# Zero-padding the 64-row and 33-row matmuls of a two-block sequence model to 128 rows, with two more pages of SBUF

## The chip, the cores and the metric

One core of a Trainium2 chip runs the whole program. The metric is the device time of one execution in microseconds; the kernel before was run three times, with a median of 2347.4 us. A core has TensorE (matmuls into PSUM, each preceded by a load of its stationary operand), VectorE, ScalarE and GpSimd (elementwise work), and a queue, SyncE, that issues most of the DMAs. SBUF has 128 partitions; a matmul contracts over the partitions, so "rows" below means the partitions that its two operands span.

## What is computed

512 tokens of width 1024 (float32) go through two blocks of two layers each. Cut to what the change touches, the reference is

```python
# first block, each layer: h = rmsnorm(x) @ w_in, cut into heads
#   sliding-window attention with sinks: 4 query heads of 64, 2 key heads of 64
scores = einsum('bnqhgd,bnkhd->bnhgqk', qb, kk) * (d ** -0.5)
#   stick-breaking attention: 4 heads of 64
z = einsum('bqhd,bkhd->bhqk', qblk, kf) * scale
# second block, each layer: 8 query heads and 2 key heads of 64, 512 tokens and 256 context tokens
s = einsum('bqhgd,bkhd->bhgqk', q, k) * (HEAD_DIM ** -0.5)
# second block's long convolution: its filter comes from a small network over 33 position features
h = sin(fr1 * (z @ w1 + b1));  h = sin(fr2 * (h @ w2 + b2));  h = h @ w3     # 33 -> 64 -> 64 -> 512
```

The rest is projections, a latent attention, a gated convolution, Fourier mixing, the modulation of the second block by a condition, and convolved feed-forward halves.

## The kernel before

The program is one straight list of instructions, traced from Python generators that `weave` interleaves: attention steps beside projections that fill TensorE. A scheduler then sets each engine's order from the instructions' dependences, so neighbours in the code are not always neighbours on TensorE.

Large products are split products (`mm3`, lines 559 to 561): each float32 operand is held as a high and a low part of a type that TensorE takes in one pass, and three matmuls over 128 rows give high*high, high*low and low*high. Small products are done directly in float32, which the trace shows as two passes each.

Heads have 64 features, so some products span 64 rows:

- `stick` (line 924): two heads stand in the two halves of the partitions of one tile, keys `qk[2 * pr + 1]` and queries `qk[2 * pr]`; head `hh` uses rows `64 * hh` to `64 * hh + 64` of both.
- `swa` (line 1060): the two key heads are the two halves of one tile; query head `h` uses half `h // 2`.
- `filter_nets` (line 1172) contracts over the 33 position features, then over 128 rows that hold both layers' hidden units; `filters` (line 1198) takes one layer's 64 rows.
- `Mix.attend` (lines 1892 and 1893), the second block's scores: queries are stored as high and low parts stacked on the partitions, and the high keys `kh` twice over, so one 128-row matmul (line 1892) gives both parts of the query times the high key. The low keys `kl` are stored once, two heads in the two halves, and a 64-row matmul (line 1893) adds the high query times the low key into the same PSUM bank. There are 8 (query tile, head pair) steps for the context, one key segment each, and in each layer 16 for the tokens, with a segment of 512 and one of 256 keys; each step has two heads, which makes 144 matmuls on each of the two lines. Behind the scores come VectorE's maximum (line 1897), ScalarE's exponential (line 1898), transposes of the weights on TensorE (line 1919), copies out of PSUM (line 1924), and the products with the values (`pv_pair`, lines 886 and 887), which put two heads side by side in two halves of TensorE's columns.

The modulation's products (line 1303) use a quarter of the columns each. `Mix.keys` (line 1716 on) makes `kh`, `kl` and the values of a token tile; line 1736 copies `kl`. `dense` makes the first block's queries and keys, one ScalarE copy out of PSUM for each tile of 128 features.

SBUF is handed out by `Arena`: 24 pages of columns, `PAGES`, each of which holds one type at a time. A first trace records when each buffer is needed, `place` assigns pages and columns, and `spread` moves buffers so that there is a pause before columns are used again. GpSimd does the `rstd` of every norm (lines 568 and 569), two small instructions in its queue.

Of the kernel before, what the change touches and what calls it, by code (L numbers as in the profile page):

```python
# [12 lines left out]
ALU = mybir.AluOpType  # L13
# [15 lines left out]
# ---------------------------------------------------------------- first block: column layout  # L29
# [20 lines left out]
def tiles_a(w, cols):  # L50
    """[K, N] -> [len(cols), 128, K/128 * 128]: one column group of 128 in each unit."""
    k = w.shape[0] // P
    out = w[:, np.concatenate([np.asarray(c) for c in cols])]
    out = out.reshape(k, P, len(cols), P).transpose(2, 1, 0, 3)
    return np.ascontiguousarray(out.reshape(len(cols), P, k * P))


def tiles_b(w, per):
    """[K, N] -> [K/128/per, 128, per * N]: `per` row groups of 128 in each unit."""
# [5 lines left out]
def cols128(v):  # L65
    """[n * 128] -> [128, n]"""
# [28 lines left out]
# The second block's input projection, by feature: queries, keys, values, the Fourier part, and the  # L95
# six tiles of the long convolution in the order in which they are used.
# [7 lines left out]
def dft_tables():  # L104
    """Tables that depend on the shapes alone: transforms, filter positions and decay, rotations."""
    out = {}
    f = np.float32
    for tag, n in (("x", S), ("c", C)):
        nt = n // P
        ht = nt // 2  # L110
        # Odd multiples of half a bin, by halves: the frequencies k and n - 1 - k share all but signs,
        # and even and odd times go apart.
# [3 lines left out]
        # [frequency tile, time in the tile, time tile, (re, im), frequency]  # L116
        fwd = np.stack([np.cos(ang), -np.sin(ang)]).reshape(2, ht, P, nt, P).transpose(1, 4, 3, 0, 2)
        out["fwd_" + tag] = np.ascontiguousarray(fwd.reshape(ht, P, nt * 2 * P).astype(f))
        if n == S:
            # [frequency tile, frequency, (re, im), time]  # L120
            inv = np.stack([np.cos(ang), -np.sin(ang)]).reshape(2, ht, P, n).transpose(1, 2, 0, 3)
        else:
            # [frequency or its mirror, frequency, (re, im), time]
# [14 lines left out]
        out["hyz_" + tag] = np.ascontiguousarray(z.T.astype(f))  # L138
# [21 lines left out]
def pack2(g, a):  # L160
# [5 lines left out]
    # What the modulation's rows take: the bias, and for the two gates the gains that go with them.  # L166
# [16 lines left out]
    # Both layers' filter networks side by side.  # L183
    hw = np.zeros((P, 772), f)
    for l in two:
# [3 lines left out]
        hw[ls, 260:772] = g["hy_w3_2"][l]  # L189
# [30 lines left out]
def pack(inp):  # L220
    """Lays the inputs out for the chip: no arithmetic."""
# [37 lines left out]
def weave(*streams):  # L259
    """Traces generators side by side: next comes the one that is least far on. A stream is a  # L260
    generator of costs and their expected sum."""
# [15 lines left out]
PAGES = [2048] * 23 + [720]  # L277
# [14 lines left out]
class Arena:  # L292
    """Columns of SBUF, handed out and taken back as the program is traced: what is read and written
# [1910 lines left out]
```

## Time and profile before

| | |
|---|---|
| runs | 2347.40, 2346.09, 2356.58 us, median 2347.4 us |
| profiled execution: span of its instructions | 2345.5 us; its own time is not given apart, the median of the runs is 1.9 us above the span |
| TensorE busy | 2251.5 us, 96% |
| VectorE, ScalarE, GpSimd busy | 1409.6, 1017.0 and 219.5 us |
| granted TensorE clock, mean | 0.982 of full speed |
| DMA | 235.33 MB, 100 GB/s |

Busy time counts the union of an engine's instructions. The ends of matmuls are modelled, and neighbours overlap in the records, so for TensorE the distance from one start to the next tells more than a duration does. PE is TensorE, PEld its weight loads, DVE VectorE, ACT ScalarE, POOL GpSimd. In a matmul's shape "64*128 64x512" the first number is the rows, the second the columns of the stationary operand, the last the columns that stream.

### The profile page before, as it was taken

To read this page: it belongs to the slowest core of one execution; us is meant where nothing else is said; L and a number is where in the kernel's file an instruction comes from. 1 tells how busy PE (TensorE), PEld (TensorE's weight loads), DVE (VectorE), ACT (ScalarE), POOL (GpSimd) and SP (SyncE) were. 2 spreads that over 40 slices of the span, in tenths; PEclk is the share of its full clock that TensorE was granted. 3 is DMA by queue.
4 is the path that set the end of the run, shared out by engine and by line. 5 is a ranking of instruction groups with operands and counts; after the bars stand their busy time and mean duration, and the time that the engine had idled before them with its cause. 6 is when DMAs were issued, how large, how long until landed. Compare 5 with 4: busy or idle time off the path is not lost.

```text
span 2345.5 us, 31203 instructions
## 1 busy us (share of the span) xinstructions
PE 2251.5 (96%) x12119; PEld 1755.1 (75%) x12122; DVE 1409.6 (60%) x2480; ACT 1017.0 (43%) x1896; POOL 219.5 (9%) x368
## 2 busy tenths in 40 slices
PE   7999999999999989999999999999889999999997
PEld 6545678755577777678988888888677778888886
DVE  4665675346666465565755655655866556566565
ACT  4345444255346335665532332223545555433332
POOL 1052002021012100010000000000320001000001
PEclk9989999999999989999999999999899999999999
DMA  5566423455531123213211221212134022233221
GB/s 167 184 205 195 154 85 93 132 177 175 158 110 54 55 68 124 88 47 116 76 56 45 81 72 54 72 54 83 46 108 135 28 89 83 73 107 108 99 90 63
DMA packets 72396, 235.33 MB, mean 100 GB/s; under 512 B 9046, under 2 KB 11031, under 8 KB 72248
## 3 DMA queue, kind: packets, MB, share of 16 engines
q1 hardware_dynamic: 65392, 223.06, 29.4%
q10 hardware_dynamic: 6856, 10.27, 1.4%
q8 instruction: 95, 1.56, 0.3%
q14 instruction: 53, 0.43, 0.1%
HBM read 224.82 MB, written 8.49 MB: 99 GB/s over the span
## 4 chain that ended last, share of the span: by engine, by line
PE 60%; DVE 6%; DMA 4%; ACT 3%; POOL 2%; issue 1%; DVEq 0%; POOLq 0%; ACTq 0%; SPq 0%
PE f L560 9%; PE f L559 9%; PE f L561 9%; PE b L559 7%; PE b L561 7%; PE b L560 7%; PE f L1893 2%; PE b L1919 2%; PE f L1892 2%; DVE page L528 2%; PE b L887 2%; POOL small L569 1%; ACT page L527 1%; PE b L886 1%; DMA page<-b_up 1%
## 5 line engine op out<-in xcount | busy, mean ns | idle before, releaser
L527 ACT ACTIVATE page<-page 128x1024 fp32r<-128x1024 f32 (+7 forms) x472 | 393.3, 846 | 631.9 <-PE f L560 158.1
L528 DVE TENSOR_TENSOR page<-page,page 128x1024 fp32r<-128x1024 f32 (+7 forms) x472 | 450.4, 967 | 324.5 <-ACT page L527 308.7
L559 PE MATMUL f<-page,page 128*128 128x512 f32 (+2 forms) x1456 | 522.4, 361 | 11.5 <-ACT page L527 10.7
L560 PE MATMUL f<-page,page 128*128 128x512 f32 (+2 forms) x1452 | 525.2, 362 | 6.5 <-DVE page L528 6.4
L561 PE MATMUL f<-page,page 128*128 128x512 f32 (+2 forms) x1452 | 519.3, 359 | 0.0
L559 PE MATMUL b<-page,page 128*128 128x512 f32 (+3 forms) x1352 | 511.5, 379 | 6.1 <-ACT page L527 2.0
L560 PE MATMUL b<-page,page 128*128 128x512 f32 (+3 forms) x1356 | 503.4, 372 | 2.2 <-DVE page L528 2.1
L561 PE MATMUL b<-page,page 128*128 128x512 f32 (+3 forms) x1356 | 501.8, 371 | 0.0
L559 PEld LDWEIGHTS f<-page,page 128*128 128x128 f32 x1456 | 275.6, 190 | 56.3 <-ACT page L527 14.6
L560 PEld LDWEIGHTS f<-page,page 128*128 128x128 f32 x1452 | 276.2, 190 | 48.0 <-DVE page L528 11.2
L559 PEld LDWEIGHTS b<-page,page 128*128 128x128 f32 x1352 | 256.4, 190 | 69.9 <-issue 21.1
L561 PEld LDWEIGHTS f<-page,page 128*128 128x128 f32 x1452 | 275.0, 190 | 39.5 <-DVE page L528 1.5
L560 PEld LDWEIGHTS b<-page,page 128*128 128x128 f32 x1356 | 257.5, 190 | 48.9 <-issue 9.0
L561 PEld LDWEIGHTS b<-page,page 128*128 128x128 f32 x1356 | 257.2, 190 | 44.4 <-issue 6.3
L568 POOL TENSOR_SCALAR small<-small 128x1 f32<-128x1 f32 (+3 forms) x104 | 37.6, 361 | 1417.5 <-ACT page L1335 529.5
L2054 DVE TENSOR_TENSOR page<-b,page 128x512 f32<-128x512 f32 x148 | 100.5, 688 | 83.6 <-PE b L561 83.6
L1382 ACT ACTIVATE page<-f,page 128x512 f32<-128x512 f32 (+1 forms) x128 | 89.2, 696 | 116.8 <-PE f L561 116.7
L1897 DVE TENSOR_REDUCE small<-f 128x1 f32<-128x768 f32 (+1 forms) x80 | 67.3, 848 | 51.2 <-PE f L1893 50.2
L569 POOL TENSOR_TENSOR small<-small,nhalf 128x1 f32<-128x1 f32 (+3 forms) x104 | 87.0, 837 | 8.6
L1383 DVE SCALAR_TENSOR_TENSOR page<-f,page,page 128x511 f32<-128x511 f32 (+1 forms) x84 | 57.1, 679 | 48.3 <-ACT page L1382 48.3
L1924 ACT ACTIVATE page<-b 128x512 f32<-128x512 f32 x104 | 59.0, 597 | 36.8 <-PE b L1919 36.4
L1898 ACT ACTIVATE page<-f,small 128x768 f32<-128x768 f32 (+1 forms) x80 | 65.0, 815 | 16.0 <-DVE small L1897 15.2
(297 smaller groups left out, 2510.4 us busy)
## 6 DMA issues: line engine op xcount, KB each, us to landing
page<-w_mod SPq DMA_DIRECT2D x96, 512.0 KB, 3.9
page<-b_up SPq DMA_DIRECT2D x88, 512.0 KB, 3.4
page<-b_dn SPq DMA_DIRECT2D x44, 512.0 KB, 3.8
page<-b_wa SPq DMA_DIRECT2D x42, 512.0 KB, 5.1
page<-b_wo SPq DMA_DIRECT2D x40, 512.0 KB, 3.4
page<-b_wq SPq DMA_DIRECT2D x14, 512.0 KB
page<-b_wkvf SPq DMA_DIRECT2D x12, 512.0 KB, 3.5
page<-b_wp SPq DMA_DIRECT2D x12, 512.0 KB, 4.1
```

The lines of the kernel that those rows point to most:

```text
L527: nc.scalar.activation(h, src, AF.Copy)
L528: nc.vector.tensor_tensor(l, src, h.bitcast(F32), op=ALU.subtract)
L559: first = nc.tensor.matmul(out, lhsT=ah, rhs=bh, start=start, stop=False, skip_group_check=skip)
L560: nc.tensor.matmul(out, lhsT=ah, rhs=bl, start=False, stop=False, skip_group_check=skip)
L561: nc.tensor.matmul(out, lhsT=al, rhs=bh, start=False, stop=stop, skip_group_check=skip)
L569: nc.gpsimd.tensor_tensor(r, r, self.nhalf[:, :n], op=ALU.pow)
L1382: nc.scalar.activation(o, ps, AF.Identity, scale=taps[:, 1:2], bias=taps[:, 3:4])
L1383: nc.vector.scalar_tensor_tensor(o[:, 1:], ps[:, : n - 1], taps[:, 0:1], o[:, 1:], op0=ALU.mult, op1=ALU.add)
L1897: nc.vector.tensor_reduce(mx, s, axis=AX.X, op=ALU.max, negate=True)
L1898: nc.scalar.activation(p, s, AF.Exp, bias=mx, accum_out=zs[i][:, 2 * j + hh : 2 * j + hh + 1])
L1924: nc.scalar.activation(o, pt, AF.Copy)
L2054: nc.vector.tensor_tensor(o, ps, o, op=ALU.add)
```

## The change

Every operand of 64 or 33 rows gets 128 rows, with zeros where another head's or no data stands, and its matmul runs over all rows.

- Stick and sliding-window scores: the queries (stick) and the keys (sliding window) are kept in a tile of twice the columns, `zeroed()`: for each of two heads its own rows hold data and the other 64 are cleared by GpSimd. `apart` writes the two halves out of PSUM, one by ScalarE, the other by VectorE, where one ScalarE copy wrote both.
- Second block: `kl` becomes two tiles, one for each key head, with the other head's rows cleared; its copy out of PSUM becomes two copies of 64 rows. The query side stays as it is, so that its other part meets zeros.
- Filters: the third weights of the two layers stand in separate columns with zeros in the other layer's rows (1284 columns in place of 772), and the positions have 128 rows in DRAM, 95 of them zeros.
- SBUF: the scratch for DMA descriptors is made smaller, and `PAGES` goes from 23 of 2048 columns and one of 720 to 25 of 2048 and one of 400.

```diff
-        out["hyz_" + tag] = np.ascontiguousarray(z.T.astype(f))
+        out["hyz_" + tag] = np.zeros((P, n), f)
+        out["hyz_" + tag][:33] = z.T
...
-    hw = np.zeros((P, 772), f)
+    hw = np.zeros((P, 260 + 512 * DEPTH), f)
...
-        hw[ls, 260:772] = g["hy_w3_2"][l]
+        hw[ls, 260 + 512 * l : 772 + 512 * l] = g["hy_w3_2"][l]
...
-PAGES = [2048] * 23 + [720]
+PAGES = [2048] * 25 + [400]
...
-            nc.scalar.dma_start(self.hyz[:33, c], self.d["hyz_" + tag])
+            nc.scalar.dma_start(self.hyz[:, c], self.d["hyz_" + tag])
...
-        self.sbqk = [self.new(S) for _ in range(4)]
+        self.sbqk = [self.new(S) if j % 2 else self.zeroed() for j in range(4)]
...
-            nc.scalar.activation(self.sbqk[j], ps, AF.Copy, scale=0.125 if j % 2 == 0 else 1.0)
+            if j % 2:
+                nc.scalar.activation(self.sbqk[j], ps, AF.Copy)
+            else:
+                self.apart(self.sbqk[j], ps, 0.125)
...
-        self.swqk = [self.new(S) for _ in range(3)]
+        self.swqk = [self.new(S), self.new(S), self.zeroed()]
...
-            nc.scalar.activation(self.swqk[j], ps, AF.Copy)
+            if j < 2:
+                nc.scalar.activation(self.swqk[j], ps, AF.Copy)
+            else:
+                self.apart(self.swqk[j], ps)
...
+    def zeroed(self):
+        a = self.new(2, S)
+        for j in range(2):
+            self.nc.gpsimd.memset(a[64 - 64 * j : 128 - 64 * j, j], 0.0)
+        return a
+    def apart(self, out, ps, scale=1.0):
+        for j in range(2):
+            rows = slice(64 * j, 64 * j + 64)
+            if j == 0:
+                self.nc.scalar.activation(out[rows, j], ps[rows], AF.Copy, scale=scale)
+            else:
+                self.nc.vector.tensor_scalar(out[rows, j], ps[rows], scale, None, op0=ALU.mult)
...
-                nc.tensor.matmul(z, lhsT=qk[2 * pr + 1][rows, kt * P : kt * P + P], rhs=qk[2 * pr][rows, kt * P :], start=True, stop=False, skip_group_check=True)
+                nc.tensor.matmul(z, lhsT=qk[2 * pr + 1][:, kt * P : kt * P + P], rhs=qk[2 * pr][:, hh, kt * P :], start=True, stop=False, skip_group_check=True)
...
-                nc.tensor.matmul(s, lhsT=qk[j][rows, i * P : i * P + P], rhs=qk[2][rows, w0 : w0 + 256], start=True, stop=True)
+                nc.tensor.matmul(s, lhsT=qk[j][:, i * P : i * P + P], rhs=qk[2][:, g, w0 : w0 + 256], start=True, stop=True)
...
-            nc.tensor.matmul(ps, lhsT=self.hya[rows, at + t * P : at + t * P + P], rhs=self.hyw[rows, 260:], start=True, stop=True)
+            nc.tensor.matmul(ps, lhsT=self.hya[:, at + t * P : at + t * P + P], rhs=self.hyw[:, 260 + 512 * l : 772 + 512 * l], start=True, stop=True)
...
-        self.kv = new(2, n, dt=F32R), new(n, dt=F32R), new(nt, P)
+        self.kv = new(2, n, dt=F32R), new(2, n, dt=F32R), new(nt, P)
+        for g in range(2):
+            nc.gpsimd.memset(self.kv[1][64 - 64 * g : 128 - 64 * g, g].bitcast(F32), 0.0)
...
-        nc.vector.tensor_copy(kl[:, ts], pt[:, 256:384])
+        for j in range(2):
+            rows = slice(64 * j, 64 * j + 64)
+            nc.vector.tensor_copy(kl[rows, j, ts], pt[rows, 256:384])
...
-                    nc.tensor.matmul(o, lhsT=qt[hh][rows, j, ts], rhs=kl[rows], start=False, stop=True)
+                    nc.tensor.matmul(o, lhsT=qt[hh][:, j, ts], rhs=kl[:, hh], start=False, stop=True)
...
-    nc = _bacc.Bacc("TRN2", target_bir_lowering=False, num_devices=1)
+    nc = _bacc.Bacc("TRN2", target_bir_lowering=False, num_devices=1, dynamic_dma_scratch_size=1024)
```

TensorE has as many instructions as before, in a somewhat other order. In the second block's first token attention it stood as follows before; 1892 and 1893 are the scores, 1919 the transposes, 559 and 560 a split product of the long convolution.

```order
3184 L1892 MATMUL f_0_6374<-page_24_98,page_27_99 128x512
3185 L1893 MATMUL f_0_6374<-page_24_98,page_27_99 128x512
3186 L1892 MATMUL f_0_6374<-page_24_98,page_27_99 128x256
3187 L1893 MATMUL f_0_6374<-page_269_4700,page_27_99 128x256
3188 L1919 MATMUL b_64<-ident,page_60_473 128x128 x4
3189 L1919 MATMUL b_65<-ident,page_60_473 128x128 x2
3190 L559 MATMUL b_63<-page_288_4750,page_2_86 128x256
3191 L560 MATMUL b_63<-page_288_4750,page_2_86 128x256
```

With the change the same place reads as follows; 1915 and 1916 are the scores, 1942 the transposes, 908 one half of a product with the values, 560 a split product.

```order
3184 L1915 MATMUL f_0_6403<-page_24_99,page_27_100 128x512
3185 L1916 MATMUL f_0_6403<-page_24_99,page_27_100 128x512
3186 L1915 MATMUL f_0_6403<-page_281_4718,page_27_100 128x256
3187 L1916 MATMUL f_0_6403<-page_281_4718,page_27_100 128x256
3188 L1942 MATMUL b_64<-ident,page_321_4939 128x128 x4
3189 L1942 MATMUL b_65<-ident,page_321_4939 128x128 x2
3190 L908 MATMUL b_66<-page_8_91,page_60_473 64x128
3191 L560 MATMUL b_63<-page_303_4935,page_326_4948 128x256
```

The scores keep their places; all four are now over 128 rows, and a product with the values has come to stand behind the transposes.

On GpSimd the clears are new. Before, the end of the first block and the first norms of the second read as follows, 568 and 569 being the two instructions of a square root.

```order
201 L568 TENSOR_SCALAR small<-small 128x4 [waits DVE_49]
202 L569 TENSOR_TENSOR small<-small,nhalf 128x4 [waits Pool_49]
203 L568 TENSOR_SCALAR small<-small 128x1 [waits DVE_49]
204 L569 TENSOR_TENSOR small<-small,nhalf 128x1 [waits Pool_49]
205 L568 TENSOR_SCALAR small<-small 128x1 [waits DVE_49]
206 L569 TENSOR_TENSOR small<-small,nhalf 128x1 [waits Pool_49]
207 L568 TENSOR_SCALAR small<-small 128x1 [waits Activation_49]
208 L569 TENSOR_TENSOR small<-small,nhalf 128x1 [waits Pool_49]
```

With the change, line 1698 being the clears of the halves of `kl`:

```order
209 L1698 MEMSET page_281_4718 64x256 [waits PE_49,Pool_49]
210 L569 TENSOR_SCALAR small<-small 128x4 [waits DVE_49,Pool_49]
211 L570 TENSOR_TENSOR small<-small,nhalf 128x4 [waits Pool_49]
212 L569 TENSOR_SCALAR small<-small 128x1 [waits DVE_49]
213 L570 TENSOR_TENSOR small<-small,nhalf 128x1 [waits Pool_49]
214 L1698 MEMSET page_24_99 64x512 [waits PE_49]
215 L1698 MEMSET page_281_4718 64x256 [waits PE_49]
216 L569 TENSOR_SCALAR small<-small 128x1 [waits DVE_49]
217 L570 TENSOR_TENSOR small<-small,nhalf 128x1 [waits Pool_49]
218 L569 TENSOR_SCALAR small<-small 128x1 [waits Activation_49]
219 L1698 MEMSET page_24_99 64x512 [waits PE_49,Pool_49]
220 L570 TENSOR_TENSOR small<-small,nhalf 128x1 [waits Pool_49]
```

Four clears stand between the square roots, each behind a wait for TensorE.

## Rows read from the trace of the kernel before

**Rows 1.** The page: span, busy time of each engine, the chain that ended last.
```profile
span 2345.5 us, 31203 instructions
PE 2251.5 (96%) x12119; PEld 1755.1 (75%) x12122; DVE 1409.6 (60%) x2480; ACT 1017.0 (43%) x1896; POOL 219.5 (9%) x368
PE 60%; DVE 6%; DMA 4%; ACT 3%; POOL 2%; issue 1%; DVEq 0%; POOLq 0%; ACTq 0%; SPq 0%
```

**Rows 2.** Busy time by window, second block's attentions: stretch, length, engines, clock, DMA share.
```profile
865.00:912.00 47.00, 43.62 (x263) 32.28 (x262) 31.82 (x69) 30.78 (x83) 1.27 (x1) 0.89 0.27 88
941.00:1051.00 110.00, 109.23 (x772) 79.99 (x772) 66.73 (x106) 70.20 (x144) 9.64 (x10) 0.98 0.19 63
1789.00:1906.00 117.00, 116.71 (x832) 85.42 (x831) 65.95 (x105) 69.94 (x146) 5.74 (x4) 1.00 0.17 57
```

**Rows 3.** Timeline of TensorE in the first token attention: start, duration, line, shape.
```profile
955.80 0.38 PE L1893 MATMUL f<-page,page 64*128 64x256 f32 x1
956.11 0.49 PE L1892 MATMUL f<-page,page 128*128 128x512 f32 x1
956.53 0.50 PE L1893 MATMUL f<-page,page 64*128 64x512 f32 x1
956.96 0.38 PE L1892 MATMUL f<-page,page 128*128 128x256 f32 x1
957.27 0.38 PE L1893 MATMUL f<-page,page 64*128 64x256 f32 x1
...
958.98 0.28 PE L559 MATMUL b<-page,page 128*128 128x256 f32 x1
959.10 0.29 PE L560 MATMUL b<-page,page 128*128 128x256 f32 x1
```

**Rows 4.** One line's instructions, line 1893: count and forms.
```profile
L1893 PE MATMUL f<-page,page x144: 378/385/792, 865.5 to 1905.5; 64*128 64x256 f32 x80, 64*128 64x512 f32 x64
```

**Rows 5.** Timeline of TensorE in the first layer's sliding-window attention.
```profile
286.93 0.40 PE L559 MATMUL b<-page,page 128*128 128x512 f32 x1
287.16 0.40 PE L560 MATMUL b<-page,page 128*128 128x512 f32 x1
287.48 0.70 PE L1060 MATMUL f<-page,page 64*128 64x256 f32 x2
288.02 0.59 PE L1060 MATMUL f<-page 64*128 64x256 f32 x2
288.54 0.51 PE L561 MATMUL b<-page,page 128*128 128x512 f32 x1
288.88 0.39 PE L559 MATMUL b<-page,page 128*128 128x512 f32 x1
```

**Rows 6.** The same view, ten microseconds later.
```profile
296.85 0.48 PE L1060 MATMUL f<-page 64*128 64x256 f32 x1
296.86 0.48 PE L1060 MATMUL f<-page,page 64*128 64x256 f32 x1
```

**Rows 7.** Busy time by window, the beginning and the stretch with the filters.
```profile
0.00:110.00 110.00, 92.16 (x482) 69.73 (x482) 63.08 (x137) 43.44 (x91) 10.91 (x30) 0.98 0.54 171
110.00:165.00 55.00, 49.92 (x203) 24.27 (x202) 33.73 (x55) 23.49 (x52) 30.91 (x48) 0.81 0.60 188
```

**Rows 8.** Groups by line and shape, VectorE and GpSimd: count, busy us, mean ns, idle before.
```profile
L521 DVE COPY page<-b 128x512 f32<-128x512 f32 x25 | 17.3, 691 | 15.5 <-PE b L561 7.5 <-PE b L1017 3.6 <-PE b L1078 2.7
L1736 DVE CAST page<-b 128x128 fp32r<-128x128 f32 x12 | 3.5, 289 | 3.0 <-ACT page L1735 2.8
L481 POOL MEMSET zb<- 128x512 bf16 x1 | 0.5, 524 | 0.0
L1202 POOL TENSOR_TENSOR page<-page,page 128x512 f32<-128x512 f32 x6 | 7.8, 1302 | 6.8 <-ACT page L1200 6.8
```

**Rows 9.** Waits of TensorE, longest first: total us, times, longest us.
```profile
PE b L593 <- DVE page L585: 13.6, 6, 11.3
```

More of the change, by code (lines that the diff above doesn't have):

```diff
@@ L725, in block1 @@
         self.rope_tables()
-        self.hyw, self.hyz = self.new(772), self.new(S + C)
+        self.hyw, self.hyz = self.new(260 + 512 * DEPTH), self.new(S + C)
         nc.scalar.dma_start(self.hyw, self.d["hyw"])
         for tag, c in (("x", slice(0, S)), ("c", slice(S, S + C))):
-            nc.scalar.dma_start(self.hyz[:33, c], self.d["hyz_" + tag])
+            nc.scalar.dma_start(self.hyz[:, c], self.d["hyz_" + tag])
         for n, ap in first.items():
@@ L921, in first @@
             for hh in range(2):
-                rows = slice(64 * hh, 64 * hh + 64)
                 z = self.pa(n)
-                nc.tensor.matmul(z, lhsT=qk[2 * pr + 1][rows, kt * P : kt * P + P], rhs=qk[2 * pr][rows, kt * P :], start=True, stop=False, skip_group_check=True)
+                nc.tensor.matmul(z, lhsT=qk[2 * pr + 1][:, kt * P : kt * P + P], rhs=qk[2 * pr][:, hh, kt * P :], start=True, stop=False, skip_group_check=True)
                 t = sp(n)
@@ L1057, in swa @@
                 g, j = h // 2, h % 2
-                rows = slice(64 * g, 64 * g + 64)
                 s = self.pa(256)
-                nc.tensor.matmul(s, lhsT=qk[j][rows, i * P : i * P + P], rhs=qk[2][rows, w0 : w0 + 256], start=True, stop=True)
+                nc.tensor.matmul(s, lhsT=qk[j][:, i * P : i * P + P], rhs=qk[2][:, g, w0 : w0 + 256], start=True, stop=True)
                 nc.vector.tensor_tensor_reduce(p[:, h], s, mask, 1.0, -3e38, op0=ALU.add, op1=ALU.max, accum_out=m[:, h : h + 1])
@@ L1167, in filter_nets @@
         a = zt
-        for j, (o, m) in enumerate(((0, 33), (128, P))):
+        for j, o in enumerate((0, 128)):
             MARK("filters")
@@ L1171, in filter_nets @@
             for b, c in zip(ps, (slice(0, S), slice(S, n))):
-                nc.tensor.matmul(b[:, : c.stop - c.start], lhsT=w[:m, o : o + P], rhs=a[:m, c], start=True, stop=True)
+                nc.tensor.matmul(b[:, : c.stop - c.start], lhsT=w[:, o : o + P], rhs=a[:, c], start=True, stop=True)
             a = zt if j == 0 else self.hya
@@ L1188, in filters @@
         nt = n // P
-        rows = slice(64 * l, 64 * l + 64)
         sd = self.dram(f"sd_{l}{tag}", (P, nt, 512))
@@ L1887, in weights @@
             for hh in range(2):
-                rows = slice(64 * hh, 64 * hh + 64)
                 w = banks().rearrange("p (a e) -> p a e", e=512) if not self.isx else banks()
@@ L2187, in plan @@
     except Traced as t:
-        return place(t.args[0])
+        log = t.args[0]
+    return place(log)
 def kernel(**inputs):
@@ L2195 @@
     arrays = pack(inputs)
-    nc = _bacc.Bacc("TRN2", target_bir_lowering=False, num_devices=1)
+    nc = _bacc.Bacc("TRN2", target_bir_lowering=False, num_devices=1, dynamic_dma_scratch_size=1024)
     dram = {n: nc.dram_tensor(n, a.shape, mybir.dt.from_np(a.dtype), kind="ExternalInput").ap() for n, a in arrays.items()}
```

## The prediction

> **What bounds the kernel now.** I read the page first. The span is 2345.5 us and TensorE is busy in 96% of it, ScalarE in 43%; the chain of waits gives TensorE 60%, and no other engine over 6% [rows 1]. So most of what shortens TensorE's stream shortens the kernel, as long as the stream is tight where the edit falls. The second view is therefore the busy time of the three stretches in which the second block's score matmuls (lines 1892 and 1893) stand: TensorE is busy 43.62 of 47 us, 109.23 of 110 and 116.71 of 117, while ScalarE works 70 us and VectorE 66 us in each of the two long ones [rows 2]. TensorE is the bound there, with 40 us of room on the next engine.
>
> The third view is TensorE's timeline inside such a stretch, and there the start times matter, not the durations, since neighbouring matmuls overlap in the records. In a plain stream of 128-row products, 256 columns start 0.12 us apart (958.98, 959.10) [rows 3] and 512 columns 0.23 us apart (286.93, 287.16) [rows 5]. In the run of scores, where 128 rows (line 1892) and 64 rows (line 1893) alternate, 256 columns take 0.31 us to the next start (955.80 to 956.11; 956.96 to 957.27) and 512 columns 0.42 to 0.43 us (956.11 to 956.53 to 956.96) [rows 3]. Each such matmul pays 0.19 to 0.20 us more than the stream. No wait is shown at these rows: the pause belongs to the change of the row count itself. A second place says the same: around a group of 64-row f32 scores of the first block the entry costs 0.32 instead of 0.23 us (287.16 to 287.48), four passes take 1.06 us (287.48 to 288.54) where four of about 0.21 would be 0.86, and the 512-column product behind them takes 0.34 instead of 0.23 (288.54 to 288.88) [rows 5]. That is 0.39 us for one change to 64 rows and one back, again 0.19 to 0.20 each. I take 0.19.
>
> **The change part by part.** *Scores of the second block.* 144 matmuls of line 1893 become 128-row ones [rows 4]. Twice the rows should cost nothing by themselves: the records give 0.38 us to 256 columns of 64 rows and of 128 rows alike, and 0.50 and 0.49 us to 512 columns [rows 3]. What goes is the change of kind. In the order of TensorE's instructions I counted neighbours that differ in kind (128 rows by 128 columns, 64 rows, 64 columns, 32 columns): in the second block's mixing stages 405 before, 146 with the change, those around the 64-column products of lines 886 and 887, which the change leaves alone. 259 fewer at 0.19 us are 49.2 us. How much of it reaches the end? After it the 110 us stretch would be near 89 us with 70 us of ScalarE work in it, so short waits for the exponentials can appear; in the 47 us stretch some waits exist already. I take 95%: **46.7 us**. If half of the pauses turned into waits it would be 25 us; the ends are 25 and 52.
>
> *First block and filters.* The 64-row scores of lines 924 and 1060, the filters of line 1198 and the 33-row ones of line 1172 become 128-row. Changes of kind in that part fall from 292 to 233: 59 at 0.19 us are 11.2 us saved. Against that, two 64-row matmuls that use different halves of the rows run on top of each other now: two L1060 passes start at 296.85 and 296.86 [rows 6]. Adding up the start times of all 148 such f32 passes, 6.0 us lie on top of each other; these become serial. Net 5.2 us on TensorE. Between 110 and 165 us it is busy only 49.92 of 55 us and its clock is 0.81 [rows 7], so not all of it counts: **4 us**, ends -5 and +10.
>
> *New work.* (a) Three outputs per layer of the first block are written in two halves, ScalarE one and VectorE the other. ScalarE's half keeps its column count, so its time. VectorE gets 6 more reads of 512 columns, at 0.69 us like the full copy of line 521 [rows 8]: 4.1 us in all, beside a VectorE that is busy 33.73 of 55 us [rows 7]. The product that needs the bank next lies 24 matmuls of 0.23 us behind, which hides them; uncovered they cost 4.1 us. (b) The low key parts are copied by halves: 12 more copies of 128 columns at 0.289 us [rows 8], 3.5 us, the same cover in the long stretches. (c) GpSimd clears halves: 16 times 512 columns and 4 times 256. No row shows an f32 clear; between the 0.524 us of a bf16 one and the 1.3 us of an f32 sum of 512 columns [rows 8] that is 9 to 23 us of an engine that is busy 9% [rows 1]. What they can hold up is what stands behind them in GpSimd's order, the square roots of the norms: two clears at each of four norms are 4 to 10 us if nothing covers them. (d) 0.26 MB more of filter weights and 0.29 MB more of filter positions arrive in the first 110 us, which move 171 GB/s at 0.54 of the DMA engines' time [rows 7]: 3.2 us of transfers, behind loads that leave room. For (a) to (d) together I take **2 us** lost, ends 0 and 20.
>
> *Two more pages.* The planner places everything anew, and the scheduler orders anew. TensorE's idle time is 94 us of the span [rows 1]; a part of it is waits for buffers. More pages could remove some, other neighbours could add some. I take **0**, ends -8 and +10: small, since the largest wait of TensorE for another engine is 13.6 us in total [rows 9].
>
> Sum: 2345.5 - 46.7 - 4 + 2 = 2296.8 us of span. The three runs have a median of 2347.4, 1.9 us over the profiled span, so the forecast of the median is **2299 us**, 2.1% less.
>
> **The rivals.**
> *The lost overlap is larger than the gain of the switches in the first block.* For it: the pair at 296.85 and 296.86 [rows 6]. If all 64 passes of line 924 (17.2 us at 0.43, 0.32, 0.22 and 0.11 us for 512 to 128 columns) and all 64 of line 1060 (13.8 us) ran in pairs, 15.5 us would be lost instead of 6.0, and the time would be 2308. Against it: the group at 287.48 [rows 5] runs its four passes one after another, at 1.06 us, and most groups look like that one. The Trainium skill advises just the opposite of this change: "TensorE: Matmul & The Clock Gate", section "Why this matters for your kernels", would have matmuls of few rows put into different row groups, to run at once. By that rule padding throws away up to half of these passes; the trace agrees for pairs that stand side by side, but line 1893 has a 128-row neighbour on both sides [rows 3] and nothing to pair with. 8%.
>
> *The next engine takes half of the gain.* In the stretches of scores ScalarE has the exponentials and the copies of the transposed weights. If its 70 us [rows 2] fall unevenly, TensorE stalls behind each softmax, and half of the 49 us come back as waits: 2321. For it: in the first, short stretch TensorE is idle 3.4 us already [rows 2]. Against it: other products of the layer are woven between the steps, and 19 us of room remain. 12%.
>
> *The pauses are not due to the row count.* They could come from two matmuls adding into one bank, or from loading the same weights twice; then the change saves nothing there, loses the overlap and adds the new work: 2347.4 + 6 + 2 = 2355. Against it: three passes of a split product also add into one bank and share weights, at 0.12 and 0.23 us [rows 3, 5]. 3%.
>
> *Slower than before: the clears block the norms.* The clears of the key halves wait for TensorE to finish with the old contents of their columns, and stand ahead of a norm's square root on GpSimd. If a clear is placed on columns that are read late, the norm, its transposes and TensorE wait. GpSimd's order has seven such places, two in each layer of the first block and three where the second block's mixing halves begin; TensorE's present waits for norms are the 13.6 us for line 585, the longest of 11.3 [rows 9]. From 7 us at each of the seven the 49 us are gone; at 11 us each, 28 us more, the time is 2375. For it: such clears stand directly before square roots in the order shown above. Against it: the planner keeps a pause behind freed columns. 3%.
>
> **How the numbers follow.** 74% for the forecast, whose own range is 2284 to 2313: 46.7 may be 52 or 38, the first block +4 or -5, the new work 0 to 8, the pages -8 to +10, and the clock, granted at 0.81 and 0.89 in two stretches [rows 2, 7], can give back or cost some 5 us. With the second rival up to 2321 the range that should hold 8 in 10 is 2283 to 2321. A measurement of this kernel tells about 0.5% from no change, that is 11.7 us: faster than 2335.7 is 93%, within is 4%, slower than 2359.1 is 3%.
>
> **What would show it.** Right: starts of scores 0.23 us (512) and 0.12 us (256) apart; the two long stretches shorter by some 20 us each, with TensorE still over 95% busy; no matmul of 64 or 33 rows left, and no pairs of starts 0.01 us apart in lines 924 and 1060. Wrong: score starts still 0.31 and 0.43 apart; new waits of TensorE for ScalarE in these stretches of over 10 us; waits for the norms of over 20 us in sum.

## The result, and the profile after

The changed kernel takes 2298.25 us (median of 4 runs, 2295.85 to 2299.32); the kernel before took 2350.44 us beside it (4 runs, 2346.09 to 2356.58). The ratio is 0.978, 95% interval 0.976 to 0.980: 2.2% faster. The forecast was 2299 us. The total came out; two of its terms did not, and the experiments show that they missed in opposite directions.

The profiled execution took 2299.32 us, its span is 2297.3 us, 48.2 us less than [rows 1]. The page of the changed kernel, its span, its busy times and the chain that ended last:

```profile
span 2297.3 us, 31229 instructions
...
PE 2193.8 (95%) x12119; PEld 1748.6 (76%) x12122; DVE 1418.7 (62%) x2498; ACT 1015.2 (44%) x1896; POOL 231.6 (10%) x388
...
PE 61%; DVE 6%; ACT 3%; POOL 3%; DMA 2%; issue 1%; POOLq 0%; DVEq 0%; ACTq 0%
```

TensorE lost 57.7 us of busy time with the same 12119 instructions, but the span fell by only 48.2: TensorE's idle time grew from 94.0 to 103.5 us. VectorE gained 18 instructions and 9 us, GpSimd 20 and 12 us, and neither matters in what follows.

TensorE's timeline in the first token attention (start, duration, line, shape, idle time before and what ended it); lines 1915 and 1916 are the scores that were 1892 and 1893:

```profile
945.83 0.50 PE L1915 MATMUL f<-page,page 128*128 128x512 f32 x1 [0.37 <-ACT page L1921]
946.17 0.40 PE L1916 MATMUL f<-page,page 128*128 128x512 f32 x1
946.41 0.28 PE L1915 MATMUL f<-page,page 128*128 128x256 f32 x1
946.52 0.28 PE L1916 MATMUL f<-page,page 128*128 128x256 f32 x1
...
946.87 0.40 PE L1915 MATMUL f<-page,page 128*128 128x512 f32 x1
947.10 0.40 PE L1916 MATMUL f<-page,page 128*128 128x512 f32 x1
```

Where [rows 3] had 0.42 us to the next start for 512 columns and 0.31 for 256, there are now 0.23 to 0.24 (946.17 to 946.41; 946.87 to 947.10) and 0.11 us (946.41 to 946.52), the distances of the plain stream. The first row is new in another way: TensorE waited 0.37 us for ScalarE's exponential, and the start behind it comes 0.34 us later. The Trainium skill, "TensorEngine Tiling (Array Packing)", section "Key Properties", says that a change of tiling mode drains TensorE; the trace agrees: where the changes of row count stood, [rows 3] has about 0.19 us more from start to start.

Busy time by window, from the first score of a mixing half to the norm of the feed-forward behind it (window, length, then busy time of PE, PEld, DVE, ACT, POOL, the granted clock, DMA share, GB/s). The kernel before:

```profile
865.50:1066.90 201.40, 195.84 (x1299) 147.52 (x1299) 125.82 (x208) 122.47 (x261) 13.28 (x14) 0.96 0.27 87
1747.40:1956.90 209.50, 208.74 (x1300) 160.30 (x1301) 126.52 (x194) 114.39 (x216) 14.18 (x16) 1.00 0.27 86
```

The changed kernel, the same two stretches and the short context part at the head of the first:

```profile
856.80:1041.10 184.30, 169.55 (x1303) 141.96 (x1302) 125.76 (x212) 121.68 (x262) 14.17 (x14) 0.97 0.29 94
1716.90:1909.60 192.70, 189.00 (x1298) 157.38 (x1299) 128.01 (x195) 114.82 (x216) 13.33 (x16) 0.99 0.30 96
...
856.80:902.00 45.20, 34.78 (x258) 29.40 (x257) 34.31 (x75) 30.28 (x81) 2.86 (x2) 0.91 0.26 88
```

The stretches are 17.1 and 16.8 us shorter. TensorE's idle time in them grew from 5.6 to 14.8 us and from 0.8 to 3.7 us. Most of it stands in the context part, 10.4 idle us of 45.20, where the kernel before had 3.4 of 47 [rows 2]. The remaining 14.3 us of the 48.2 lie outside these two stretches: 8.7 ahead of the first, 4.7 between them and 0.9 behind the second.

One piece inside runs at the full clock in both kernels and nearly without waits: the second layer's token scores, from the first to the last. The kernel before, then the changed one:

```profile
1788.90:1905.60 116.70, 116.41 (x832) 85.25 (x830) 66.05 (x105) 70.04 (x146) 5.74 (x4) 1.00 0.17 57
1759.90:1858.30 98.40, 96.92 (x831) 81.66 (x830) 66.51 (x105) 70.32 (x146) 5.74 (x4) 1.00 0.24 81
```

The records have 167 changes of kind there before and 54 after. The 113 that went made TensorE's busy time 19.5 us shorter, 0.17 us each.

TensorE's waits over the whole changed kernel (who waited, for whom: total us, times, longest):

```profile
PE b L594 <- DVE page L586: 18.4, 8, 11.9
...
PE b L1455 <- DVE page L522: 6.4, 2, 5.1
PE f L1915 <- ACT page L1921: 5.2, 8, 1.9
```

The wait for norms is 18.4 us, 4.8 more than [rows 9], and its longest is nearly the same. The wait of the scores for the exponentials is 5.2 us.

The groups that the change added, on VectorE and ScalarE (line, operation, count, busy us, mean ns, idle time before):

```profile
L819 DVE TENSOR_SCALAR page<-b 64x512 f32<-64x512 f32 x6 | 4.2, 695 | 0.2
L817 ACT ACTIVATE page<-b 64x512 f32<-64x512 f32 x6 | 3.4, 573 | 0.0
```

and on GpSimd, the clears:

```profile
L810 POOL MEMSET page<- 64x512 f32 x12 | 6.3, 521 | 26.7 <-issue 15.7 <-PE f L562 6.5 <-PE b L562 3.9
L1698 POOL MEMSET page<- 64x512 f32 x4 | 2.1, 520 | 507.2 <-PE f L562 506.0 <-PE f L561 1.1
L1698 POOL MEMSET page<- 64x256 f32 x4 | 1.2, 307 | 0.2
```

A clear of 512 columns takes 0.52 us, the lower of the two bounds taken from [rows 8]; all 20 take 9.6 us.

### The profile page after: what moved, and what is told of

Read it like the earlier page. It is cut to its first block, busy times and chain, and to the rows that moved or that the text cites. A ratio compares the mean times of both kernels' runs of the same rounds, so it can differ in the third digit from the quotient of the medians.

```text
span 2297.3 us, 31229 instructions
## 1 busy us (share of the span) xinstructions
PE 2193.8 (95%) x12119; PEld 1748.6 (76%) x12122; DVE 1418.7 (62%) x2498; ACT 1015.2 (44%) x1896; POOL 231.6 (10%) x388
## 4 chain that ended last, share of the span: by engine, by line
PE 61%; DVE 6%; ACT 3%; POOL 3%; DMA 2%; issue 1%; POOLq 0%; DVEq 0%; ACTq 0%
PE f L561 10%; PE f L560 10%; PE f L562 10%; PE b L560 8%; PE b L562 7%; PE b L561 7%; POOL small L570 2%; PE b L1942 2%; PE b L909 2%; DVE page L529 1%; PE f L1915 1%; PE b L908 1%; ACT page L528 1%; PE f L1916 1%; POOL small L569 1%
## 5 line engine op out<-in xcount | busy, mean ns | idle before, releaser
L1402 DVE SCALAR_TENSOR_TENSOR page<-f,page,page 128x511 f32<-128x511 f32 (+1 forms) x128 | 84.0, 656 | 69.8 <-ACT page L1401 69.7
L1403 DVE SCALAR_TENSOR_TENSOR page<-f,page,page 128x511 f32<-128x511 f32 (+1 forms) x128 | 84.3, 659 | 3.7
L1322 PE MATMUL b<-page,page 128*32 128x256 f32 x768 | 64.1, 396 | 7.1 <-DMA page<-w_mod 6.9
```

Of the source, the lines that this page charges most:

```text
L1402: nc.vector.scalar_tensor_tensor(o[:, 1:], ps[:, : n - 1], taps[:, 0:1], o[:, 1:], op0=ALU.mult, op1=ALU.add)
L1403: nc.vector.scalar_tensor_tensor(o[:, : n - 1], ps[:, 1:], taps[:, 2:3], o[:, : n - 1], op0=ALU.mult, op1=ALU.add)
```

## The experiments

The theory at the start was that of the prediction: each change of TensorE between 128-row and 64-row products costs 0.19 us, and the change removes them. The rivals were the pages, the placement, the clears, ScalarE's copies, and a cause of the pauses other than the rows. Kernels are named by their edit against the kernel before or against the changed one; each was timed beside the kernel before on its own chip, and the ratio is to that.

### The pages alone

The kernel before, with

```diff
-PAGES = [2048] * 23 + [720]
+PAGES = [2048] * 25 + [400]
-    nc = _bacc.Bacc("TRN2", target_bir_lowering=False, num_devices=1)
+    nc = _bacc.Bacc("TRN2", target_bir_lowering=False, num_devices=1, dynamic_dma_scratch_size=1024)
```

> The kernel before with the smaller scratch and 25 pages of 2048 and one of 400, nothing padded. Theory A (each change of kind on TensorE costs 0.19 us, pages are neutral): 2345 to 2355 us. Theory B (the gain outside the second block's attention, some 14 us in the traces, comes from the pages): 2334 to 2342 us.

Measured: 2352.05 us (12 runs, 2347.24 to 2360.9) against 2348.49 (23 runs), ratio 1.002 (1.0005 to 1.0036). The pages by themselves give nothing, and may cost some 3 us. They are what makes room for the padded tiles.

### The second block's scores alone

New pages, and of the padding only `kl`, in two tiles:

```diff
-                    nc.tensor.matmul(o, lhsT=qt[hh][rows, j, ts], rhs=kl[rows], start=False, stop=True)
+                    nc.tensor.matmul(o, lhsT=qt[hh][:, j, ts], rhs=kl[:, hh], start=False, stop=True)
```

> New pages, and only the second block's low keys padded (lines 1893 of before become 128 rows; first block and filters stay at 64 and 33). Theory A: the traces of before and after put 33.9 us between the first context score and the next norms of the two layers, so 2312 to 2320 us, 30 to 38 us under before. Theory B: the same 34 us plus the pages' share, 2302 to 2309 us.

Measured: 2315.9 us (4 runs, 2310.24 to 2316.6), ratio 0.985 (0.984 to 0.987): 32.6 us. This is the main part, and it is smaller than the 46.7 us that the prediction gave it.

### The first block and the filters alone

New pages and all the padding but that of `kl`.

> New pages, and only the first block and the filters padded; the second block's scores stay at 64 rows. Theory A: 59 changes of kind less at 0.19 us against 6.0 us of lost overlap, minus some for waits: 3 to 8 us under before, 2342 to 2347 us. Theory B: 12 us or more under before, at most 2338 us, and no faster than the pages alone.

Measured: 2337.95 us (12 runs, 2327.15 to 2350.51), ratio 0.995 (0.994 to 0.997): 10.5 us faster than the kernel before, 14 less than the pages alone. That is more than the 3 to 8 us of theory A, and theory B does not fit either, since the pages alone give nothing. The two parts, 32.6 and 10.5, make 43 of the 52 us by which the kernel got faster.

The spread of 23 us needed an explanation. Its profiled execution was the longest of the twelve. One window of 99 us each, beginning 4 us behind the first context score in this kernel:

```profile
863.60:962.60 99.00, 94.59 (x467) 70.74 (x469) 55.59 (x96) 50.56 (x115) 4.41 (x6) 0.76 0.27 88
```

and 2 us behind it in the kernel with the pages alone:

```profile
872.00:971.00 99.00, 92.80 (x557) 68.65 (x557) 65.11 (x107) 59.72 (x137) 4.41 (x6) 0.97 0.31 99
```

Both issue the same matmuls there in the same order, with the 64-row low-key scores left in. One was granted 0.76 of the clock and got 467 matmuls done, the other 0.97 and 557. That execution lost 15 us between the first context score and the last token score; its mean clock was 0.978, and the execution of 2327 us had 0.987. The two kernels with 128-row low-key scores shown so far ran within 6.4 and 3.5 us, in 4 runs each.

### A different order of the same rows

The kernel before, without padding and with the old pages. In a step with two key segments, both 128-row products of a head now come first and both 64-row ones behind them, which takes the changes of kind in the second block's mixing from 405 to 314:

```diff
                     nc.tensor.matmul(o, lhsT=qt[hh][:, j, ts], rhs=kh[:, hh], start=True, stop=False)
+                for seg, (kh, kl, _) in enumerate(kvs):
+                    o = w[:, seg, : nk[seg] * P]
                     nc.tensor.matmul(o, lhsT=qt[hh][rows, j, ts], rhs=kl[rows], start=False, stop=True)
```

> The kernel before, nothing padded, pages as before; only the order of a head's score matmuls is altered: first both key segments with the high keys (128 rows), then both with the low keys (64 rows). In TensorE's order the changes of kind in the second block's mixing fall from 405 to 314. Theory A (the price is 0.19 us for each change of kind): 91 times 0.19 is 17 us, less some quarter for waits as in the changed kernel: 2331 to 2338 us. Rival (the 64-row matmul itself is what is slow, or what zeros free): no difference, 2345 to 2352 us.

Measured: 2330.94 us (6 runs, 2328.67 to 2334.8) against 2348.02 (11 runs), ratio 0.993 (0.991 to 0.994): 17.1 us. The 91 changes that went, at 0.19 us, are 17.3. That the two lie so close is partly chance: in the profiled executions 2.8 us of the gain arise between 105 and 212 us, where nothing was edited and the granted clock was 0.92 in place of 0.89. The second layer's token scores show the price by themselves. They are 8.4 us shorter than before, with 121 changes in place of 167, 0.18 us each:

```profile
1780.20:1888.50 108.30, 107.44 (x832) 81.91 (x830) 66.10 (x104) 70.24 (x146) 5.75 (x4) 1.00 0.19 62
```

TensorE's timeline of this kernel at the same place ("x2" are two matmuls in one row of the view; 1892 has 128 rows, 1895 has 64):

```profile
956.25 0.51 PE L1892 MATMUL f<-page,page 128*128 128x512 f32 x2
956.69 0.61 PE L1895 MATMUL f<-page,page 64*128 64x512 f32 x2
957.23 0.62 PE L1892 MATMUL f<-page,page 128*128 128x512 f32 x2
957.78 0.50 PE L1895 MATMUL f<-page,page 64*128 64x512 f32 x1
```

The pair of 128-row products, 512 and 256 columns, needs 0.44 us without a change before it (956.25 to 956.69) and 0.55 us with one (957.23 to 957.78), where the plain stream needs 0.35. No row was padded and the arithmetic is the same, so it is not the 64 rows that are slow. Nor is it the shared bank: each key segment has a bank of its own, so in this order no neighbours among the scores add into one bank, and the pauses still stand at the changes. In the changed kernel neighbours do share bank and weights, and start at the plain distances. The pause belongs to the change of kind, which settles the third rival.

### What the planner's knobs are worth

Every edit of this program makes the planner place anew, so some runs ask what that alone does. First, the changed kernel with another pause behind freed columns:

```diff
-'pause': 200
+'pause': 150
```

> The changed kernel with one number of the placing altered (the wished pause before columns are used again is 150 instructions in place of 200); arithmetic and padding are the same. If placing and the order that follows from it are worth little: within 3 us of the changed kernel's 2298 us. If they alone move some 5 to 10 us, differences of that size between the other kernels can't be put down to their edits: 2288 to 2293 or 2303 to 2308 us.

Measured: 2302.75 us (4 runs, 2298.77 to 2306.65), ratio 0.980 (0.978 to 0.982). 4.5 us is what a mere change of place does, so differences of this size between kernels can't be put down to their edit.

Then the weights with which attention is woven into the other work, `'att': 0.7` in the changed kernel, with the totals of the streams changed to match. First 0.8:

> The changed kernel with the weaving altered: an attention step counts 0.8 instead of 0.7 for each key tile, in the step and in its stream's total, so that more of the other products stand between two steps. If TensorE waits in the scores because the filling products between the steps are too few now that a step is shorter: 3 to 8 us under the changed kernel, 2290 to 2296 us. If the filling is only moved and is missing elsewhere: 2296 to 2306 us.

Measured: 2308.64 us (4 runs, 2306.03 to 2313.42), ratio 0.983 (0.981 to 0.985), 10 us slower than the changed kernel. In its profile the loss arises at the second block's first norms (700 to 760 us), where 13.7 us were granted the half clock and one wait of 5.0 us is new. Behind them the parts differ both ways: the part with the context's scores is 9 us shorter, the first layer's other token scores are 8 us longer. Then 0.6:

> The changed kernel with the weaving altered the other way: an attention step counts 0.6 instead of 0.7 for each key tile. With 0.8 the time was 10 us longer, most of it where the norms of the second block begin and in the attentions. If the count matters by the amount of filling between steps, less filling means more waits for the exponentials: 2301 to 2308 us. If the 10 us came from where the planner and the scheduler happened to put things: anywhere within 10 us of 2298, with the attentions' own stretches within 3 us of the changed kernel's.

Measured: 2300.32 us (5 runs, 2298.96 to 2301.16), ratio 0.978 (0.976 to 0.980): the changed kernel's own ratio.

### ScalarE's share of the weight copies

In the changed kernel the first group of four transposed weights of each step is copied by VectorE in place of ScalarE:

```diff
-'pv': 0
+'pv': 1
```

> The changed kernel, where the first of a step's three copies of transposed weights (512 columns) goes from ScalarE to VectorE. If the part of the scores' gain that did not arrive (about 13 us) is TensorE waiting for ScalarE's exponentials, ScalarE being the late one: 3 to 8 us under the changed kernel, 2290 to 2296 us. If it is the step's latency, whichever engine carries it, or VectorE is as late: within 3 us or slower, 2296 to 2306 us.

Measured: 2311.67 us (4 runs, 2308.09 to 2312.26), ratio 0.984 (0.982 to 0.985): slower than the changed kernel by 13 us. A miss: unloading ScalarE did not help. In its profile TensorE's wait for the exponentials rose from 5.2 to 6.8 us, and between the first token score of the first layer and its last one 17.1 us were granted the half clock, against 3.4 us in the changed kernel. Since the weaving alone moved the time by 10 us, the 13 us can't be put down to the copies themselves.

### The clears on VectorE

```diff
-            self.nc.gpsimd.memset(a[64 - 64 * j : 128 - 64 * j, j], 0.0)
+            self.nc.vector.memset(a[64 - 64 * j : 128 - 64 * j, j], 0.0)
...
-            nc.gpsimd.memset(self.kv[1][64 - 64 * g : 128 - 64 * g, g].bitcast(F32), 0.0)
+            nc.vector.memset(self.kv[1][64 - 64 * g : 128 - 64 * g, g].bitcast(F32), 0.0)
```

> The changed kernel with all 20 clears on VectorE instead of GpSimd. If clears in GpSimd's queue hold up the norms' square roots (TensorE's waits for norms are 18.4 us after and 13.6 us before): 3 to 5 us under the changed kernel, 2293 to 2296 us. If they hold up nothing: within 3 us, or a little slower because VectorE is the busier engine, 2296 to 2303 us.

Measured: 2300.24 us (5 runs, 2297.31 to 2303.84), ratio 0.980 (0.978 to 0.981), within 2 us of the changed kernel. With no clear left in GpSimd's queue nothing gets faster, so the clears hold up no norm.

### The stick scores back to 64 rows

The changed kernel with the queries of `stick` unpadded, as before; everything else stays padded:

```diff
-        self.sbqk = [self.new(S) if j % 2 else self.zeroed() for j in range(4)]
+        self.sbqk = [self.new(S) for _ in range(4)]
...
-                nc.tensor.matmul(z, lhsT=qk[2 * pr + 1][:, kt * P : kt * P + P], rhs=qk[2 * pr][:, hh, kt * P :], start=True, stop=False, skip_group_check=True)
+                nc.tensor.matmul(z, lhsT=qk[2 * pr + 1][rows, kt * P : kt * P + P], rhs=qk[2 * pr][rows, kt * P :], start=True, stop=False, skip_group_check=True)
```

> The changed kernel with the stick-breaking scores at 64 rows again, so that heads can run on top of each other; all else padded. TensorE's order has 26 changes of kind more (4.9 us at 0.19), and 3.8 us of overlap come back (line 924 in the trace of before). Theory A: 0 to 3 us over the changed kernel, 2298 to 2301 us. Rival (the overlap that padding gives up is worth more than the changes of kind): 2290 to 2295 us.

Measured: 2315.94 us (4 runs, 2314.13 to 2316.7), ratio 0.985 (0.983 to 0.987): 17.7 us slower than the changed kernel, a miss for both theories. Read naively, padding these 64 passes would be worth more than a third of the whole gain. Setting the two traces side by side, landmark by landmark, says otherwise. The first and last stick scores of layer 0 stand at 108.2 and 206.5 us in the changed kernel, and at 108.4 and 207.3 here; the last sliding-window score at 298.1 and 298.4. Only then does it fall behind: the first norm of layer 1 starts at 366.2 and 376.5 us. Of the 16.3 us by which its span is longer, 10 arise in this one place, where no stick score stands, and 2.4 more in the norm behind it.

TensorE's timeline there, with 64-row stick scores (1151 sums the last group's squares, 1169 spreads its scale):

```profile
332.51 0.40 PE L562 MATMUL b<-page,page 128*128 128x512 f32 x1
335.75 1.98 PE L1151 MATMUL b<-ones,page 128*128 128x128 f32 x8 [2.85 <-POOL page L1147]
340.76 0.79 PE L1169 MATMUL b<-page,ones 128*128 128x512 f32 x1 [3.03 <-ACT page L531]
...
346.93 0.63 PE L561 MATMUL f<-page,page 128*128 128x512 f32 x1
347.36 0.63 PE L562 MATMUL f<-page,page 128*128 128x512 f32 x1
```

and in the changed kernel, whose lines are 1153 and 1171:

```profile
336.40 1.16 PE L1153 MATMUL b<-ones,page 128*128 128x128 f32 x8 [1.05 <-POOL page L1149]
337.31 0.71 PE L562 MATMUL f<-page,page 128*128 128x512 f32 x2
...
340.58 0.50 PE L1171 MATMUL b<-page,ones 128*128 128x512 f32 x1 [0.71 <-ACT page L531]
```

The scaling needs the sum, by way of GpSimd, VectorE and ScalarE. In the changed kernel ten products of the output projection stand between them; in this one none do. TensorE waits 2.85 and 3.03 us, and from the end of the first wait on it is granted the half clock, for 13.7 us. The window of that time (the 0.50 is the granted clock):

```profile
335.90:349.50 13.60, 9.14 (x24) 6.58 (x25) 7.44 (x10) 5.84 (x7) 1.21 (x2) 0.50 0.33 105
```

Products of 512 columns start 0.43 us apart (346.93 to 347.36) in place of 0.23. In the 30 us from 320 on TensorE issues 83 matmuls here and 126 in the changed kernel; 43 at 0.23 us are 9.9 us.

### Cover and rows taken apart

The output projection of layer 0 is cut in two, with work of the next norm between. Cutting it after 2 features in place of 3,

```diff
-'cut0': 3
+'cut0': 2
```

happens to bring those products back between sum and scaling when the stick scores have 64 rows, and to take them away when they have 128. So the same edit on both kernels separates the cover from the rows.

> The changed kernel with the first block's stick scores over 64 rows again, as before, and the layer's output projection cut after 2 of its 8 input features in place of 3, which brings a dozen products back between the last group's square sum and its scaling at the end of the first layer; with the cut at 3 the 64-row stick scores leave none there. Theory (the loss with 64-row stick scores is that bare wait and the half clock behind it, not the scores themselves): 2298 to 2306 us, TensorE's wait between the two under 2 us, no half clock near 340 us. Rival (128-row stick scores are worth 17 us by themselves): 2312 to 2320 us.

Measured: 2296.04 us (4 runs, 2293.47 to 2299.31) against 2349.91 (7 runs), ratio 0.977 (0.974 to 0.979).

> The changed kernel, all padded, with the output projection of the first layer cut after 2 in place of 3; here this cut takes the products away from between the last group's square sum and its scaling. Theory (a bare wait there costs some 10 us, whatever the scores' rows): 2305 to 2315 us, three waits of TensorE of 3 us each near 335 us and some 14 us of half clock. Rival (the rows of the stick scores decide): 2296 to 2302 us.

Measured: 2314.09 us (4 runs, 2313.32 to 2317.53), ratio 0.985 (0.982 to 0.988).

| | products between sum and scaling | none |
|---|---|---|
| stick scores over 128 rows | 2298.25 | 2314.09 |
| stick scores over 64 rows | 2296.04 | 2315.94 |

Down the columns the rows make 2 us, of either sign; across, the cover makes 16 to 20. The theory held in both, though the first came in 2 us below its range. The same place in the trace with 64-row scores and the cut at 2:

```profile
332.59 1.16 PE L1151 MATMUL b<-ones,page 128*128 128x128 f32 x8 [0.75 <-POOL page L1147]
...
336.78 0.51 PE L1169 MATMUL b<-page,ones 128*128 128x512 f32 x1 [0.72 <-ACT page L531]
```

and with everything padded and the cut at 2:

```profile
335.63 2.08 PE L1153 MATMUL b<-ones,page 128*128 128x128 f32 x8 [2.84 <-POOL page L1149]
340.73 1.52 PE L1171 MATMUL b<-page,ones 128*128 128x512 f32 x2 [3.02 <-ACT page L531]
```

The waits and the half clock go with the order and not with the rows. The kernel before has this place covered too, by nine products, so the cover is no part of what the change brought; it could have been a loss. The kernel with the other pause had it bare as well (none between, 13.7 us at the half clock), gained 6 us ahead of it, and so ended only 4.5 us behind.

The kernel with 64-row stick scores and the cut at 2 is the lowest of all, 2 us below the changed one, but the intervals (0.974 to 0.979 and 0.976 to 0.980) overlap, and a change of place is worth as much: no version is shown to beat the changed kernel.

## Why the prediction was right, and which terms were off

**The bound and the price per change** held. TensorE's stream was the limit, and the 0.19 us for each change of kind, read from start times, was confirmed by the reordering without padding: 17.1 us measured against 17.3 worked out, and 0.18 us each where nothing else differs. The starts came as forecast, and no matmul of 64 or 33 rows is left in the trace. "Some 20 us" in each long stretch came as 13.5 us (108.9 to 95.4, with 14 more matmuls of other lines in it) and 18.3 us, with TensorE busy 96% and 98%.

**The term of the second block's scores was too large.** The step that failed is "I take 95%" of the 49.2 us. The two stretches got 33.9 us shorter, and the run with these scores alone 32.6 us, which is 66 to 69%. Most of the missing part is in the trace. 257 of the changes lie in these two stretches, 48.8 us at 0.19. TensorE's idle time grew by 9.2 and 2.9 us; the half clock was granted for 6.8 us less in the first stretch and 3.4 us more in the second, which together gives back some 1.7. That would leave 38.4. At the 0.17 us that padding saved for each change in the second layer's token scores, the 257 are 43.7 us, and 33.3 are left against the measured 33.9. Why a change that is padded away gives a little less than one that is reordered away, no run shows. The short context part, of which the prediction said that "some waits exist already", is where most of the idle time arose: 7.0 us of the 12.1, with waits for the queries' copies and for exponentials.

**The second rival** (half of the gain comes back as waits) therefore happened in small: a quarter came back, not half. It came back less as a steady lag of ScalarE than as single waits, and handing part of ScalarE's copies to VectorE brought no gain.

**The first block's term was too small.** Forecast 4 us; measured 10.5 against the kernel before, and 14.3 us of the span lie outside the second block's scores. The padding of the stick scores is no part of it: 2298.25 with and 2296.04 without, which agrees with the count made ahead of that run, 26 changes gained (4.9 us) against 3.8 us of overlap lost. What remains is the sliding-window scores, the filters and the order that the planner happened to find, and no run separates these three. Laid side by side matmul by matmul, the traces place most of it all the same. The stretch with the filters and the first layer's stick scores, between 105 and 212 us, gains nothing: it is 2.8 us longer. At the first layer's sliding-window scores the changed kernel gains 2.0 us, and so it does in the other two pairs of traces that differ in this padding; at those of the first block's second layer it gains next to nothing. 5.0 us arise at one place near 388 us, where no operand of 64 or 33 rows stands. The kernel before waits there for a split of operands by VectorE,

```profile
388.19 0.71 PE L560 MATMUL f<-page,page 128*128 128x416 f32 x1 [3.24 <-DVE page L528]
```

and was granted the half clock for 6.8 us; the changed kernel has neither, and with the pages alone the wait is 1.0 us. 5.6 us more lie between and behind the two stretches of scores, where no matmul was padded. The clock is part of this: a mean of 0.982 over 2345.5 us and of 0.985 over 2297.3 us, between full and half, make some 84 and 69 us at the half clock, an estimate of 7 to 8 us for the whole kernel at half a microsecond lost in each. The pages alone already move single landmarks by up to 10 us and end level, and a bare place costs 16 to 20. Most of this remainder, then, belongs to no row count.

**The new work** cost nothing that can be seen, where 2 us were taken: the clears took 0.52 us each and moving them changed nothing, the halves on VectorE took 0.695 us as read from the full copy (0.69), and the twelve more copies of key halves 0.288 us each; the trace shows no engine waiting for any of them. **The pages** gave 0, as taken, or -3.

**The other rivals.** The lost overlap: for the stick scores it did not matter, for with 13 pairs of starts back within 0.05 us of each other the time is the same; the 8 such pairs of the sliding-window scores were not put back. A cause other than the rows' change: excluded by the reordering. Clears blocking norms: excluded by the run with VectorE, and no wait of TensorE for a norm grew past 11.9 us.

So the forecast of 2299 was right partly by compensation: 13 us too much for the scores and some 10 too little for the rest. That the two errors nearly cancel is luck. Its range, 2283 to 2321, holds every variant of the fully padded kernel that ran, 2298 to 2314, which is a fair picture of what the planner alone could have done.

## What to carry to other kernels

Look at the distance between starts on TensorE where products of different row counts alternate: here each change cost 0.17 to 0.19 us, and grouping the products by kind or padding the smaller operand with zeros removes it. Padding paid where each 64-row product stood between 128-row neighbours; for the stick scores, some of which ran in pairs over both halves, it made no difference that shows. And before a difference of some 15 us is put down to an edit, line up landmarks of the two traces: in a planned program it may arise somewhere else, at a place where the edit only happened to take the cover away.

## What the runs showed that was not expected

**Reordering alone gets a third of the gain**: 17.1 us without a column of SBUF more.

**Two bare waits of 3 us cost 10 us at their place.** With nothing to do between the last group's sum and its scaling TensorE stood still for 2.85 and 3.03 us, and from the end of the first wait on the granted clock was at half for 13.7 us; the three kernels that left this place bare all show 13.7 us there, and the changed kernel and the fastest run, which cover it, none. The kernel before shows the same in small at 388 us: 3.24 us of waiting, 6.8 us at half. The Trainium skill, "TensorE: Matmul & The Clock Gate", section "Why this matters for your kernels", warns of idle gaps on TensorE between bursts of matmuls; the trace agrees: 13.7 us at the half clock around waits of 2.85 and 3.03 us.

**The clock also moves the same program.** With the 64-row low-key scores in, one kernel's runs spread from 2327 to 2350 us, and its mean granted clock from 0.987 to 0.978. Why the clock fell in one execution and not in another of the same program, none of these runs shows.
